# S5 rotation tables of a two-layer encoder: one outer product of two power tables in place of seven doublings

## The chip, the cores and the metric

The kernel runs on one core of one Trainium2 chip. The metric is the device time of one execution in microseconds (us). The engines are named as in the profile: PE (matrix products), DVE and POOL (elementwise work), ACT (activations and copies), SP (issues most DMAs). Each engine takes its instructions in the order in which they stand in its own queue; an instruction that waits for a semaphore holds up all that stand behind it on that engine.

## What is computed

An encoder of two layers over 800 tokens of 1024 features. Each layer mixes the tokens with three groups of heads (RG-LRU, HGRN2, S5), multiplies by w_out, and adds a squared-ReLU MLP:

```python
def linear_scan(a, b, reverse): ...            # h_t = a_t * h_{t-1} + b_t

def s5_branch(u, a_re, a_im, log_dt, b_re, b_im, c_re, c_im, d_skip, glu_w, glu_b):
    ...
    for d in range(2):
        lam = lax.complex(a_re[d], a_im[d])
        dt = jnp.exp(log_dt[d])[:, None]
        a_bar = jnp.exp(lam * dt)
        b_bar = ((a_bar - 1.0) / lam)[..., None] * lax.complex(b_re[d], b_im[d])
        bu = jnp.einsum('btgh,gph->btgp', ug, b_bar)
        h = linear_scan(jnp.broadcast_to(a_bar, bu.shape), bu, reverse=(d == 1))
        y = y + jnp.real(jnp.einsum('btgp,ghp->btgh', h, c))
    ...
# layer: x += W_out [ rms(RG-LRU) | rms(HGRN2) | rms(S5) ] * gain
#        x += relu(rms(x) W_up)^2 W_down
```

The kernel runs S5 in 100 chunks of 8 tokens. The state of each chunk is rotated by a power of a unit phasor, so that the scan over the chunks has a real decay. The powers 0 to 99 of that phasor, for 16 pairs of directions and group pairs, are the **rotation tables**.

## The kernel before

Features lie on the 128 partitions and tokens along the free dimension. The large products (`product`, L428 to L439) run as three passes of 128x128 weights over 400 tokens (L434, L435, L436), with 24 matmuls for one half of an output tile, into one of three PSUM banks (tag `mm`). Every half is evacuated by an elementwise instruction: L464 (DVE) for the products with w_in, L1123 (ACT) and L1124 (DVE) for the up products of the MLP, L1150 (DVE) for its down products. PE can't write a bank again before its evacuation has run, and with three banks it is soon that far. Weights arrive as f32 (`wr`, L446) and are split by ACT (L419) and POOL (L420, 128x1024). In the MLP, POOL also does L1129 (128x800).

`s5_setup(l)` (L706 to L874) makes the constant matrices of the S5 heads of layer l from the parameters and writes them to DRAM (TB, E, F and W). That of layer 0 is issued beside the first w_in products, between about 30 and 135 us. That of layer 1 is issued within the MLP of layer 0, after the down products of its first block (`issue_after`, L1178), and lies between about 660 and 742 us. Its parts, in order: the step's powers `PW` and the doubled powers `pw[1]`, `pw[2]` to `pw[64]` (16 columns each); the input matrices `BB`; the rotation tables; the load of the output parameters `CL` (eight DMAs, L823); `BD` and the matrices E, F and W, in which PE transposes `CL` (L836) and multiplies F (L862).

`cmul` (L725) is one complex product of elementwise instructions: four products (L726 to L729), a difference (L730) and a sum (L731). The rotation tables (L795 to L816) are made in four sets, two directions by two halves of the groups. A set has two memsets (L800, L801) for power 0, and then seven doublings: the powers n to 2n-1 are the powers 0 to n-1 times `pw[n]`, by a `cmul` on 4 x m elements (m = 1, 2, 4, 8, 16, 32, 36), 42 instructions in all. In layer 0 the last set runs on POOL and all the others run on DVE. Then two DMAs write the set (L810), and L813 to L816 make and write the scan's decay `dec`.

```python
n = 1
while n < NCH:
    m = min(n, NCH - n)
    cmul(tb[n:n+m], tb[0:m], pw[n], big, ...)   # in short
    n *= 2
```

All these tiles come from one pool, tag `t`: 11 buffers of 576 floats while the setups run. A tile that takes a buffer over waits until the last reader of its former tile is done, a DMA's landing too.

The order of the instructions on each engine is not written out by hand. A list scheduler sets it ahead of time, from the program's order with some offsets (`PR`; the setup of layer 0 has one of 400 steps) and a model of the durations. A change in the number of instructions thus moves other work in the queues, too.

Of the kernel before, what the change touches and what calls it, by code (L numbers as in the profile page):

```python
"""Two-layer bidirectional encoder trunk (RG-LRU | HGRN2 | S5 head groups, squared-ReLU MLP).

Both sequences run together with features on partitions and the 800 tokens (528 + 272, each with its 16 meta
tokens first) along the free dimension. The large products run as three float32r passes over operands split
exactly into two parts; everything else is float32. HGRN2 decays are products over dyadic intervals, so that
every factor is at most one; S5 runs in chunks of 8 tokens with a rotated real scan over the chunks.
"""
# [26 lines left out]
NCH = 100  # L34
# [9 lines left out]
# order in which the parts of a layer's mixers are issued  # L44
# [18 lines left out]
# per layer: what is moved in the issue order, pools of SBUF in their order, tiles of rs, hd, hs and ra, parts that  # L63
# take their tiles elsewhere, outputs that stay on chip, groups merged in w_out's first pass, engines
# [11 lines left out]
class Trunk:  # L76
# [14 lines left out]
    def phase(self, name, tags, tmp, bank):  # L91
        """SBUF of a phase: tag -> (floats per partition, buffers); tmp and bank: what the shared parts use."""
# [36 lines left out]
    def setup(self):  # L129
        nc = self.nc  # L130
# [15 lines left out]
        # level masks: the highest bit in which s and t differ  # L146
# [12 lines left out]
        # scores of a chunk pair, block-diagonal: the blocks beside the diagonal stay zero  # L159
# [4 lines left out]
        # what leaves the chip for a while  # L164
# [7 lines left out]
    def params(self):  # L172
        nc, ident = self.nc, self.ident
        # parameter rows of 128, transposed into columns
# [9 lines left out]
        # s5 skip gains: (g2 h) rows, (l gp) columns  # L184
        r = self.s((16, 32))
# [5 lines left out]
        # s5 step sizes over the states  # L191
# [9 lines left out]
        # lower bounds: softmax over the depth, running sum less the first  # L201
# [13 lines left out]
        # forget gate = hA*t + hB, key/2 = -hK*t + hK, with t = tanh(x/2)  # L215
# [6 lines left out]
        # rg-lru: softplus(-lambda) with log1p by its atanh series  # L222
# [23 lines left out]
    def gate_weights(self, l):  # L246
        """Block-diagonal gates: (i, d, r|i)."""
# [27 lines left out]
    def load(self):  # L275
        """The residual and the operands of the first w_in, half by half of the tokens."""
# [17 lines left out]
        for b, parts in enumerate(((0, 1, 2, 3), (4, 0, 5, 6))):  # L294
            sl = slice(b * 400, b * 400 + 400)
            # the tokens' sums of squares, from the partitions to the free dimension
# [28 lines left out]
    def final(self, m, t):  # L325
        """The last norm, feature tile by feature tile as they are done."""
# [45 lines left out]
    def split(self, k, y, gain, rs=None, n=T):  # L372
        """Operand k = y*gain (*rs) as two float32r parts that add up to it exactly."""
# [12 lines left out]
    def sumsq(self, ys, n=T):  # L386
        """The sum of squares over the partitions of all tiles, on every partition: two PSUM halves."""
# [38 lines left out]
    def product(self, w, xs, halves, evac):  # L426
        """evac(half, psum) with psum = sum over k of w[k].T @ x[k]; w: pairs of [128, 128] parts."""
# [13 lines left out]
    def fetch(self, name, l, c):  # L441
        """128 columns of a weight matrix of 1024 rows, split."""
# [8 lines left out]
    def project(self, l, cols, evacs):  # L451
        """Columns of w_in, 128 from each of cols."""
# [7 lines left out]
    def scaled(self, out):  # L460
        """Evacuation into out, times the tokens' 1/rms."""
        def ev(b, ps):
            sl = slice(b * 400, b * 400 + 400)
            self.nc.vector.tensor_tensor(out=out[:, sl], in0=ps, in1=self.r1[:, sl], op=MULT)  # L464
        return ev

    def gelu(self, x):
        """x becomes 2 gelu(x), by the tanh formula."""
# [766 lines left out]
```

## Time and profile before

| what | value |
|---|---|
| timed runs | 2216.07, 2198.86, 2207.92 us; median 2207.92 us |
| span of the profiled execution | 2201.6 us |
| PE busy | 2087.4 us, 95% of the span |
| DVE, POOL, ACT busy | 1118.9, 811.9, 753.8 us |
| PE's share of the chain that ended last | 60% |
| DVE's share of that chain | 10% |

The span of the profiled execution lies 6.3 us below the median of the timed runs, and these spread over 17 us. Times below are microseconds from the start of the profiled execution. "Pitch" means the time from the start of one instruction to that of the next on the same engine; the durations that the trace gives are longer, since neighbours overlap.

### The profile page before, as it was taken

Reading aid. Unit: us, or ns where it says so; the run is one execution under the profiler, and the core shown is the slowest. Engines: PE = TensorE matmul, PEld = TensorE weight load, DVE = VectorE, ACT = ScalarE, POOL = GpSimd, SP = SyncE. Lnnn points to the kernel's source line nnn. Section 1 sums busy time; section 2 is a strip of 40 time slices with the busy share of each in tenths; the row PEclk is TensorE's granted clock in tenths of the full one; section 3 lists DMA queues with packets and bytes.
Section 4 is the critical chain, followed back from the end, with each engine's and each line's share of the span. In section 5 each row is a group of like instructions: output and inputs, shape, how many; then the busy total and the mean of one; then the engine's idle time right before and its main releaser. Section 6 shows DMA issues by size and latency. Waiting matters only on the chain.

```text
span 2201.6 us, 34495 instructions
## 1 busy us (share of the span) xinstructions
PE 2087.4 (95%) x14082; PEld 1957.7 (89%) x14082; DVE 1118.9 (51%) x2258; ACT 753.8 (34%) x1141; POOL 811.9 (37%) x622
## 2 busy tenths in 40 slices
PE   8899899889989899999999999998998999999998
PEld 6889897677979899999998879886888999999997
DVE  6884748487657871221155855746368221112224
ACT  6233535454322232212225553436432122222222
POOL 1672112263433443333444213322434343434343
PEclk9899899899999999999999999998999999999998
DMA  5322111342211431122122113221321112122221
GB/s 182 96 81 76 38 40 56 101 129 57 68 48 58 109 119 58 58 64 61 58 95 78 57 37 97 74 59 48 113 79 58 58 58 68 59 67 65 60 67 68
DMA packets 230886, 160.74 MB, mean 73 GB/s; under 512 B 33270, under 2 KB 217784, under 8 KB 230728
## 3 DMA queue, kind: packets, MB, share of 16 engines
q1 hardware_dynamic: 229832, 156.95, 23.8%
q8 instruction: 111, 1.82, 0.4%
q10 hardware_dynamic: 896, 1.58, 0.2%
q14 instruction: 47, 0.39, 0.1%
HBM read 131.32 MB, written 27.18 MB: 72 GB/s over the span
## 4 chain that ended last, share of the span: by engine, by line
PE 60%; DVE 10%; ACT 2%; issue 1%; POOL 1%; DMA 1%; SPq 0%; DVEq 0%; POOLq 0%; ACTq 0%
PE mm L435 18%; PE mm L434 18%; PE mm L436 18%; PE hb L664 2%; PE hb L582 1%; DVE m L1163 1%; DVE h L1172 1%; PE rb L510 1%; DVE xl L379 1%; DVE m L1164 1%; DVE h L1154 1%; DVE r L1173 0%; DVE m L1124 0%; PE rb L862 0%; POOL wl L420 0%
## 5 line engine op out<-in xcount | busy, mean ns | idle before, releaser
L420 POOL TENSOR_TENSOR wl<-wr,wh 128x1024 fp32r<-128x1024 f32 (+3 forms) x214 | 479.3, 2240 | 1005.5 <-ACT wh L419 982.7
L434 PE MATMUL mm<-xh,wh 128*128 128x400 f32 (+3 forms) x2016 | 710.2, 354 | 33.1 <-DVE m L1124 11.1
L435 PE MATMUL mm<-xl,wh 128*128 128x400 f32 (+3 forms) x2016 | 713.9, 355 | 6.0 <-POOL xl L383 2.9
L436 PE MATMUL mm<-xh,wl 128*128 128x400 f32 (+3 forms) x2016 | 701.1, 349 | 0.7 <-POOL wl L420 0.5
L419 ACT ACTIVATE wh<-wr 128x1024 fp32r<-128x1024 f32 (+3 forms) x214 | 205.7, 962 | 764.9 <-PE mm L435 658.5
L434 PEld LDWEIGHTS mm<-xh,wh 128*128 128x128 f32 x2016 | 388.6, 193 | 52.7 <-DVE m L1124 14.1
L435 PEld LDWEIGHTS mm<-xl,wh 128*128 128x128 f32 x2016 | 389.1, 193 | 18.5 <-DVE xl L379 4.1
L436 PEld LDWEIGHTS mm<-xh,wl 128*128 128x128 f32 x2016 | 388.8, 193 | 8.9 <-POOL wl L420 0.9
L434 PE MATMUL mm<-u,wh 128*128 128x400 f32 (+1 forms) x1024 | 349.1, 341 | 6.2 <-DVE m L1124 6.2
L435 PE MATMUL mm<-u,wh 128*128 128x400 f32 (+1 forms) x1024 | 349.6, 341 | 0.0
L436 PE MATMUL mm<-u,wl 128*128 128x400 f32 (+1 forms) x1024 | 348.3, 340 | 0.0
L1150 DVE TENSOR_TENSOR h<-mm,h 128x400 f32<-128x400 f32 (+1 forms) x256 | 144.5, 565 | 331.2 <-PE mm L436 331.2
L1124 DVE TENSOR_TENSOR m<-m,mm 128x400 f32<-128x400 f32 (+1 forms) x128 | 71.1, 559 | 369.2 <-ACT m L1123 369.2
L434 PEld LDWEIGHTS mm<-u,wh 128*128 128x128 f32 x1024 | 193.3, 189 | 7.8 <-DVE m L1124 7.1
L435 PEld LDWEIGHTS mm<-u,wh 128*128 128x128 f32 x1024 | 193.2, 189 | 0.1
L436 PEld LDWEIGHTS mm<-u,wl 128*128 128x128 f32 x1024 | 193.1, 189 | 0.1
L1129 POOL TENSOR_TENSOR u<-m,u 128x800 fp32r<-128x800 f32 (+1 forms) x64 | 127.3, 1990 | 53.5 <-ACT u L1128 45.4
L1123 ACT ACTIVATE m<-mm 128x400 f32<-128x400 f32 (+1 forms) x128 | 62.3, 489 | 129.9 <-PE mm L436 115.8
L582 PE MATMUL hb<-hs,hs 64*64 64x64 f32 x2016 | 85.7, 236 | 8.8 <-ACT hs L615 5.6
L582 PEld LDWEIGHTS hb<-hs,hs 64*64 64x64 f32 x2016 | 72.2, 146 | 24.5 <-issue 11.4
L1128 ACT ACTIVATE u<-m 128x800 fp32r<-128x800 f32 (+1 forms) x64 | 55.1, 861 | 83.1 <-DVE m L1124 73.2
L616 DVE TENSOR_TENSOR hd<-hd,hd 128x800 f32<-128x800 f32 (+2 forms) x48 | 43.1, 902 | 13.3 <-ACT hs L614 12.8
(365 smaller groups left out, 2245.8 us busy)
## 6 DMA issues: line engine op xcount, KB each, us to landing
wr<-in_w_up_dram SPq DMA_DIRECT2D x64, 512.0 KB
wr<-in_w_down_dram SPq DMA_DIRECT2D x64, 512.0 KB
wr<-in_w_in_dram SPq DMA_DIRECT2D x46, 512.0 KB
h<-h SPq DMA_DIRECT2D x16, 400.0 KB
wr<-in_w_out_dram SPq DMA_DIRECT2D x32, 192.0 KB
TB<-t SPq DMA_DIRECT2D x24, 200.0 KB
F<-t SPq DMA_DIRECT2D x16, 256.0 KB
E<-t SPq DMA_DIRECT2D x16, 256.0 KB
```

The lines of the kernel that those rows point to most:

```text
L419: self.nc.scalar.activation(hi[:], raw, AF.Copy)
L420: self.nc.gpsimd.tensor_tensor(out=lo[:], in0=raw, in1=hi[:].bitcast(F32), op=SUB)
L434: nc.tensor.matmul(ps[:, 0:n], wh, xh[:, c0 : c0 + n], start=(k == 0), stop=False)
L435: nc.tensor.matmul(ps[:, 0:n], wh, xl[:, c0 : c0 + n], start=False, stop=False)
L436: nc.tensor.matmul(ps[:, 0:n], wl, xh[:, c0 : c0 + n], start=False, stop=(k == last))
L582: nc.tensor.matmul(ps[c % 2 * 64 : c % 2 * 64 + 64, c // 2 * 64 : c // 2 * 64 + 64], K[hr, c0 : c0 + 64], Q[hr, c0 : c0 + 64], start=True, ...
L664: mm = lambda out, w, x: nc.tensor.matmul(out, w, x, start=False, stop=False, skip_group_check=True)
L1123: nc.scalar.activation(t[:, sl], ps, AF.Relu)
L1124: nc.vector.tensor_tensor(out=t[:, sl], in0=t[:, sl], in1=ps, op=MULT)
L1128: nc.scalar.activation(u[:, 0], t[:], AF.Copy)
L1129: nc.gpsimd.tensor_tensor(out=u[:, 1], in0=t[:], in1=u[:, 0].bitcast(F32), op=SUB)
L1150: mark = nc.vector.tensor_tensor(out=t[:, sl], in0=ps, in1=t[:, sl], op=ADD)
```

## The change

In place of the doublings in each set, two tables are made once for all four sets: `P1` with the powers 0 to 7 (128x2x16x8) and `P8` with the powers 0, 8, ..., 96 (128x2x16x13). They take four memsets, four copies and five `cmul` (two for P1 with 32 and 64 elements, three for P8 with 32, 64 and 80), 30 instructions. Each set is then one `cmul` of 128 x 416 elements (4 x 13 x 8; both operands are broadcast), six instructions, of which the first 100 powers of the 104 are written to TB. The one set on POOL stays on POOL. A set now takes five buffers of tag `t` (two for the table, two for temporaries, one for `dec`) in place of four, and P1, P8 and a temporary take three more. The rest of the difference between the two files blanks comments and docstrings; lines behind L816 have numbers higher by 5.

```diff
-                tb = [self.s((128, 4, NCH)) for _ in range(2)]
-                v.memset(tb[0][:, :, 0:1], 1.0)
-                v.memset(tb[1][:, :, 0:1], 0.0)
-                big = self.s((128, 2, 256))
-                n = 1
-                while n < NCH:
-                    m = min(n, NCH - n)
-                    cmul([x[:, :, n : n + m] for x in tb], [x[:, :, 0:m] for x in tb], [x[:, ds].unsqueeze(2).to_broadcast([128, 4, m]) for x in pw[n]],
-                         [big[:, i, 0 : 4 * m].rearrange("p (a b) -> p a b", b=m) for i in range(2)], (nc.gpsimd if l == 0 and d == 1 and gq == 1 else v).tensor_tensor)
-                    n *= 2
...
+        P1, P8, tp = self.s((128, 2, 16, 8)), self.s((128, 2, 16, 13)), self.s((128, 2, 128))
+        for P, w0, w in ((P1, 1, 8), (P8, 8, 13)):
+            v.memset(P[:, 0, :, 0:1], 1.0)
+            v.memset(P[:, 1, :, 0:1], 0.0)
+            for i in range(2):
+                v.tensor_copy(P[:, i, :, 1], pw[w0][i])
+            n = 2
+            while n < w:
+                m = min(n, w - n)
+                cmul([P[:, i, :, n : n + m] for i in range(2)], [P[:, i, :, 0:m] for i in range(2)], [x.unsqueeze(2).to_broadcast([128, 16, m]) for x in pw[w0 * n]],
+                     [tp[:, i, 0 : 16 * m].rearrange("p (a b) -> p a b", b=m) for i in range(2)])
+                n *= 2
...
+                tb, tm = ([self.s((128, 4, 13, 8)) for _ in range(2)] for _ in range(2))
+                cmul([x[:] for x in tb], [P8[:, i, ds].unsqueeze(3).to_broadcast([128, 4, 13, 8]) for i in range(2)], [P1[:, i, ds].unsqueeze(2).to_broadcast([128, 4, 13, 8]) for i in range(2)],
+                     [x[:] for x in tm], (nc.gpsimd if l == 0 and d == 1 and gq == 1 else v).tensor_tensor)
```

Three places in the queues. The first is DVE in layer 0, between two evacuations (L464) of w_in's products, `mm_238` and `mm_243`; `t` are tiles of the setup. Before:

```order
L464 TENSOR_TENSOR hd_234_1155<-mm_238_1184,r1_136_454 128x400 [waits PE_49]
L726 TENSOR_TENSOR t_145_594<-t_144_591,t_138_471 128x16 [waits DVE_49]
L727 TENSOR_TENSOR t_145_594<-t_143_590,t_138_471 128x16
L729 TENSOR_TENSOR t_143_590<-t_143_590,t_138_471 128x4x4
L730 TENSOR_TENSOR t_147_644<-t_147_644,t_149_648 128x4 [waits DVE_49]
L731 TENSOR_TENSOR t_148_645<-t_148_645,t_149_648 128x4
L464 TENSOR_TENSOR hd_234_1155<-mm_243_1242,r1_136_454 128x400 [waits PE_49]
```

After the change the same two evacuations are those of `mm_245` and `mm_250`:

```order
L464 TENSOR_TENSOR hd_241_1048<-mm_245_1077,r1_136_454 128x400 [waits PE_49]
L729 TENSOR_TENSOR t_144_591<-t_144_591,t_138_471 128x16x2 [waits DVE_49]
L728 TENSOR_TENSOR t_144_591<-t_144_591,t_138_471 128x16x2 [waits DVE_49]
L729 TENSOR_TENSOR t_143_590<-t_143_590,t_138_471 128x16x4 [waits DVE_49]
L464 TENSOR_TENSOR hd_241_1048<-mm_250_1135,r1_136_454 128x400 [waits PE_49]
```

Three setup instructions stand between the two evacuations in place of five; they now belong to P1 and P8.

The second place is DVE in layer 1, around the evacuations of the first half of an up product of the MLP (`mm_1126` before, `mm_1140` after; L1124, now L1129). A wait for DMAHW is one for the landing of an earlier DMA. Before:

```order
L726 TENSOR_TENSOR t_1022_6656<-t_1021_6653,t_1007_6425 128x4 [waits DMAHW3_49]
L726 TENSOR_TENSOR t_1018_6602<-t_1017_6599,t_1009_6516 128x144 [waits DVE_49]
L727 TENSOR_TENSOR t_1018_6602<-t_1016_6598,t_1009_6516 128x144
L729 TENSOR_TENSOR t_1016_6598<-t_1016_6598,t_1009_6516 128x4x36
L727 TENSOR_TENSOR t_1022_6656<-t_1020_6652,t_1007_6425 128x4
L730 TENSOR_TENSOR t_1020_6652<-t_1020_6652,t_1022_6656 128x4 [waits DVE_49]
L731 TENSOR_TENSOR t_1017_6599<-t_1017_6599,t_1018_6602 128x4x36 [waits DVE_49]
L1124 TENSOR_TENSOR m_1125_7270<-m_1125_7270,mm_1126_7271 128x400 [waits Activation_49,Pool_49]
```

After the change, up to the evacuation of the second half:

```order
L726 TENSOR_TENSOR t_1034_6514<-t_1020_6438,t_1019_6437 128x416 [waits DMAHW2_49]
L727 TENSOR_TENSOR t_1035_6515<-t_1020_6438,t_1019_6437 128x416 [waits DVE_49]
L1129 TENSOR_TENSOR m_1139_7056<-m_1139_7056,mm_1140_7057 128x400 [waits Activation_49,Pool_49]
L728 TENSOR_TENSOR t_1033_6513<-t_1020_6438,t_1019_6437 128x416 [waits DMAHW3_49]
L729 TENSOR_TENSOR t_1032_6512<-t_1020_6438,t_1019_6437 128x416 [waits DMAHW4_49]
...
L726 TENSOR_TENSOR t_1039_6531<-t_1020_6438,t_1019_6437 128x416 [waits DVE_49]
L820 MEMSET t_1036_6524 128x4 [waits DVE_49]
L820 MEMSET t_1036_6524 128x4
L727 TENSOR_TENSOR t_1040_6532<-t_1020_6438,t_1019_6437 128x416 [waits DMAHW6_49]
L1129 TENSOR_TENSOR m_1139_7056<-m_1139_7056,mm_1141_7084 128x400 [waits Activation_49]
```

The small instructions ahead of the evacuations became few large ones; in the rows shown, four of them wait for the landings of TB writes of the sets before, in place of one.

The third place is SP in layer 0, the loads of `CL` (L823, now L828) among the TB writes of the last set, the one on POOL. Before, the eight loads end ahead of it:

```order
L823 DMA t_159_806<-in_s5_c_im_dram 128x1x64 [waits DMAHW3_49]
L823 DMA t_159_806<-in_s5_c_im_dram 128x1x64 [waits DMAHW4_49]
L446 DMA wr_343_2194<-in_w_in_dram 128x8x128 [waits DMAHW5_49,Pool_49]
L810 DMA TB0_39_157<-t_155_752 128x4x100 [waits DMAHW6_49,Pool_49]
L810 DMA TB0_39_157<-t_156_753 128x4x100 [waits DMAHW7_49,Pool_49]
```

After:

```order
L815 DMA TB0_39_157<-t_162_683 128x4x100 [waits DMAHW0_49,Pool_49]
L828 DMA t_166_699<-in_s5_c_im_dram 128x1x64 [waits DMAHW1_49]
L815 DMA TB0_39_157<-t_161_682 128x4x100 [waits DMAHW2_49,Pool_49]
L828 DMA t_166_699<-in_s5_c_re_dram 128x1x64 [waits DMAHW3_49]
L828 DMA t_166_699<-in_s5_c_re_dram 128x1x64 [waits DMAHW4_49]
L828 DMA t_166_699<-in_s5_c_im_dram 128x1x64 [waits DMAHW5_49]
L828 DMA t_166_699<-in_s5_c_im_dram 128x1x64 [waits DMAHW6_49]
L446 DMA wr_350_2087<-in_w_in_dram 128x8x128 [waits DMAHW7_49,Pool_49]
```

Five of the eight loads and the next weight load now stand behind a TB write that waits for POOL.

## Rows read from the trace of the kernel before

**Rows 1.** The page: busy times of PE; the chain that ended last.
```profile
PE 2087.4 (95%) x14082; PEld 1957.7 (89%) x14082; DVE 1118.9 (51%) x2258; ACT 753.8 (34%) x1141; POOL 811.9 (37%) x622
...
PE 60%; DVE 10%; ACT 2%; issue 1%; POOL 1%; DMA 1%; SPq 0%; DVEq 0%; POOLq 0%; ACTq 0%
```

**Rows 2.** Stretches: start:end, length, busy us (instructions) by engine, PEclk, DMA.
```profile
200.00:550.00 350.00, 318.53 (x2604) 279.10 (x2602) 226.31 (x371) 169.92 (x276) 103.86 (x138) 0.93 0.23 69
715.00:770.00 55.00, 48.76 (x258) 46.58 (x257) 49.38 (x164) 10.79 (x19) 22.75 (x17) 0.91 0.42 111
825.00:880.00 55.00, 55.00 (x304) 55.00 (x303) 9.75 (x17) 12.39 (x17) 19.98 (x9) 1.00 0.20 61
1155.00:1650.00 495.00, 473.20 (x3927) 414.32 (x3926) 295.89 (x482) 229.39 (x352) 156.14 (x157) 0.96 0.24 71
```

**Rows 3.** Waits of PE, 0 to 200 us: us in total, times, longest.
```profile
PE mm L434 <- DVE t L731: 4.4, 1, 4.4
PE rb L862 <- POOL t L730: 4.0, 4, 1.7
...
PE rb L836 <- DMA t<-in_s_c_re_dram: 2.7, 1, 2.7
```

**Rows 4.** Waits of PE, 677 to 745 us (the setup of layer 1).
```profile
PE mm L434 <- DVE m L1124: 8.7, 3, 3.7
```

**Rows 5.** Timeline of DVE in layer 0: start, length, instruction.
```profile
53.53 2.36 DVE L727 TENSOR_TENSOR t<-t,t 128x16 f32<-128x16 f32 x1
...
55.90 2.31 DVE L730 TENSOR_TENSOR t<-t,t 128x4 f32<-128x4 f32 x1
...
58.20 0.56 DVE L464 TENSOR_TENSOR hd<-mm,r 128x400 f32<-128x400 f32 x1
```

**Rows 6.** Timeline of POOL in the same place.
```profile
53.50 4.69 POOL L420 TENSOR_TENSOR wl<-wr,wh 128x1024 fp32r<-128x1024 f32 x2 [5.16 <-ACT wh L419]
```

**Rows 7.** Timeline of DVE in layer 1: two setup sets interleave.
```profile
700.43 0.42 DVE L730 TENSOR_TENSOR t<-t,t 128x256 f32<-128x256 f32 x1
700.77 0.15 DVE L726 TENSOR_TENSOR t<-t,t 128x4 f32<-128x4 f32 x1
700.84 0.15 DVE L727 TENSOR_TENSOR t<-t,t 128x4 f32<-128x4 f32 x1
...
712.48 0.30 DVE L728 TENSOR_TENSOR t<-t,t 128x144 f32<-128x144 f32 x1
712.69 0.29 DVE L726 TENSOR_TENSOR t<-t,t 128x144 f32<-128x144 f32 x1
...
713.35 0.21 DVE L728 TENSOR_TENSOR t<-t,t 128x64 f32<-128x64 f32 x1
713.49 0.21 DVE L726 TENSOR_TENSOR t<-t,t 128x64 f32<-128x64 f32 x1
...
718.69 2.44 DVE L727 TENSOR_TENSOR t<-t,t 128x144 f32<-128x144 f32 x1
```

**Rows 8.** Timeline of POOL in layer 1.
```profile
718.50 2.47 POOL L420 TENSOR_TENSOR wl<-wr,wh 128x1024 fp32r<-128x1024 f32 x1
```

**Rows 9.** Timeline of PE in layer 1: two stalls, and the matmuls behind the first.
```profile
710.33 0.70 PE L434 MATMUL mm<-xh,wh 128*128 128x400 f32 x1 [2.48 <-DVE m L1124]
...
711.49 0.54 PE L434 MATMUL mm<-xh,wh 128*128 128x400 f32 x1
711.83 0.54 PE L435 MATMUL mm<-xl,wh 128*128 128x400 f32 x1
...
722.25 0.46 PE L434 MATMUL mm<-u,wh 128*128 128x400 f32 x1 [3.71 <-DVE m L1124]
```

**Rows 10.** The chain that ended last, around 715 us: start, length, what.
```profile
714.29 2.90 DMA TB<-t
717.21 1.56 DVE t L726 x2
```

**Rows 11.** Groups of POOL by shape, 70 to 135 us: busy, mean ns.
```profile
L726 POOL TENSOR_TENSOR t<-t,t 128x144 f32<-128x144 f32 x1 | 0.4, 421 | 0.0
```

More of the change, by code (lines that the diff above doesn't have):

```diff
@@ L798, in s5_setup @@
                 ds, gs = slice(8 * d + 4 * gq, 8 * d + 4 * gq + 4), slice(4 * gq, 4 * gq + 4)
-                tb = [self.s((128, 4, NCH)) for _ in range(2)]
-                v.memset(tb[0][:, :, 0:1], 1.0)
-                v.memset(tb[1][:, :, 0:1], 0.0)
-                big = self.s((128, 2, 256))
-                n = 1
-                while n < NCH:
-                    m = min(n, NCH - n)
-                    cmul([x[:, :, n : n + m] for x in tb], [x[:, :, 0:m] for x in tb], [x[:, ds].unsqueeze(2).to_broadcast([128, 4, m]) for x in pw[n]],
-                         [big[:, i, 0 : 4 * m].rearrange("p (a b) -> p a b", b=m) for i in range(2)], (nc.gpsimd if l == 0 and d == 1 and gq == 1 else v).tensor_tensor)
-                    n *= 2
+                tb, tm = ([self.s((128, 4, 13, 8)) for _ in range(2)] for _ in range(2))
+                cmul([x[:] for x in tb], [P8[:, i, ds].unsqueeze(3).to_broadcast([128, 4, 13, 8]) for i in range(2)], [P1[:, i, ds].unsqueeze(2).to_broadcast([128, 4, 13, 8]) for i in range(2)],
+                     [x[:] for x in tm], (nc.gpsimd if l == 0 and d == 1 and gq == 1 else v).tensor_tensor)
                 for i in range(2):
-                    nc.sync.dma_start(dr["TB"][gs, :, i, d].rearrange("g p c -> p g c"), tb[i][:])
+                    nc.sync.dma_start(dr["TB"][gs, :, i, d].rearrange("g p c -> p g c"), tb[i][:].rearrange("p g a b -> p g (a b)")[:, :, 0:NCH])
                 dec = self.s((128, 4, NCH))
```

## The prediction

> **What bounds the kernel now.** I read the page first, then the waits of PE in the two setup stretches, the timelines of PE, DVE and POOL there, and last the stretches beside them. PE is busy for 2087.4 of 2201.6 us and carries 60% of the chain that ended last; DVE carries 10% of it [rows 1]. So an instruction taken off DVE is worth time only where PE waits for DVE. In most of the MLP that isn't so: from 825 to 880 us PE is busy for all 55 us, with 304 matmuls, 0.181 us apart, while DVE is busy for 9.75 us [rows 2].
>
> PE does wait in the two setups. In layer 0 there is one wait of 4.4 us for a setup instruction's queue on DVE, four of 4.0 us together for POOL before L862, and one of 2.7 us for the load of CL before L836 [rows 3]. In layer 1 there are three waits for the evacuation L1124, 8.7 us together [rows 4]: 2.48 and 3.71 us [rows 9], and so 2.5 us for the third. After a wait the matmuls start 0.34 us apart for a while [rows 9] in place of 0.181: the lower of PE's two clock levels. The stretch from 715 to 770 us shows the sum, with a mean granted clock of 0.91: 258 matmuls stand in it where a full one has 304 [rows 2], and 46 x 0.181 = 8.3 us are lost, 6.2 of them in the second and third wait and about 2 in slow matmuls.
>
> What are those evacuations late for? They stand in DVE's queue behind setup instructions. Most of these are short: two of 128x4 start 0.07 us apart. But some last over 2 us: in layer 0, L727 (128x16) takes 2.36 us from 53.53, and L730 (128x4) 2.31 us from 55.90; the evacuation comes at 58.20 [rows 5]. In the same time POOL runs two L420 from 53.50, 4.69 us together [rows 6]. In layer 1, L727 (128x144) takes 2.44 us from 718.69 [rows 7], and POOL's L420 takes 2.47 us from 718.50 [rows 8]. So a DVE instruction with two SBUF inputs that meets a weight split on POOL lasts as long as the split, whatever its own size. [...]
>
> **The change part by part.** *DVE's time.* From start to start, the trace gives 0.07 us for 128x4, 0.14 for 128x64, 0.21 for 128x144 and 0.34 for 128x256 (700.43 to 700.77) [rows 7]. Between these I estimate 0.075, 0.085, 0.10 and 0.20 for 8, 16, 32 and 128 elements. A set of doublings is then 6 x (0.07 + 0.075 + 0.085 + 0.10 + 0.14 + 0.20 + 0.21) = 5.3 us, and four are 21.1 us in layer 1 and three 15.8 us in layer 0. For 128x416 I go on along the line from 4 to 256 elements, 0.27/252 us for each: 0.34 + 160 x 0.00107 = 0.51 us. Six are 3.1 us, so four sets 12.3 us and three 9.2 us. P1 and P8 cost 12 x 0.10 + 12 x 0.14 + 6 x 0.155 = 3.8 us, and with copies and memsets about 4.2 us. DVE thus saves 21.1 - 16.5 = 4.6 us in layer 1, and 15.8 - 13.4 = 2.4 us in layer 0. If the operands broadcast along the innermost dimension cost more than this, the saving is less; no row shows it for this size, but the doublings have such operands too.
>
> *Layer 0, the evacuation.* In the order of the changed kernel, three setup instructions stand between the two L464 in place of five. Of the five, two met a split each. Two splits run back to back there, so three short instructions can meet one or both; with one, DVE is done after the first split, the second evacuation starts near 56, and the wait of 4.4 us shrinks by about 2.3. Bounds: nothing gained if both are met; 4.4 us and 2 or so of slow matmuls if none. I take -2.3.
>
> *Layer 0, POOL.* One set moves from 42 small to six large instructions on POOL. A POOL instruction of 128x144 takes 0.42 us [rows 11]; in proportion, 128x416 takes 1.2 us, and six 7.3 us, less than the small ones. The F work behind it, for which L862 waits 4.0 us [rows 3], can start earlier, so up to 4.0 us may go. Against this, five of the eight CL loads now stand on SP behind a TB write that waits for POOL's set, and L836 already waits 2.7 us for CL [rows 3]: that wait may go or may double. Bounds -6.7 and +3 us; I take -1, since POOL's set ends about when the loads went out before.
>
> *Layer 1.* The last three of the setup's evacuations matter, and DVE has only saved time by the time the third wait comes: the tables (4.2 us) are made first and the long instructions of the first sets fill the places where the cheap doublings stood. Instruction by instruction along the new order, with the prices above and the splits where POOL has them now, I get waits of 2.2, 4.2 and 0.6 us, together 7.0 in place of 8.7, or -1.7. The second wait stays because a split of 2.47 us, which ends at 720.97, falls just ahead of its evacuation [rows 8]. With the third nearly gone, part of its slow matmuls goes, -0.5. What DVE saves behind 728 us is hidden: PE there has products whose evacuations aren't late. Bounds: -8.7 - 2 = -10.7 if no wait is left, and +9 for the wait under the rivals.
>
> *The rest.* Fewer instructions move the scheduler's order in both mixing stretches: S5's first tile by some thirty matmuls earlier, late HGRN work of layer 1 by as many later. PE has 350 - 318.5 = 31.5 us idle from 200 to 550, and 495 - 473.2 = 21.8 from 1155 to 1650 [rows 2], so the order matters there, and no row says which way. I take nothing, with 10 us either way as bound, a fifth of those 53.
>
> *The sum.* -2.3 - 1 - 1.7 - 0.5 = -5.5 us: the span of 2201.6 would become 2196.1. The profiled execution lies 6.3 us below the median of 2207.9, so the time is 2202.4, say 2202.
>
> **The rivals.** *Hidden* (0.20). DVE's saving falls where no evacuation is late, and as many splits are met as before. For it: DVE is 51% busy [rows 1], and a split's price doesn't depend on the instruction's size. Against it: both bracketing evacuations in layer 0 have fewer instructions between them. Time: about 2208.
>
> *All waits go* (0.12). The 4.4 and 8.7 us and the slow matmuls behind them (2 each), and L862's 4.0: -21 us, or 2187. Against it: the splits belong to the products and still come at their pace, and DVE still has 16.5 us of setup work in layer 1.
>
> *DVE waits for its own table writes* (0.10): slower. P1 and P8 stay live and a set takes five of eleven buffers in place of four, so about one set fits at a time. Its instructions then wait, in DVE's queue, for the landings of the TB writes of the set before, and evacuations stand behind them; in layer 1 the last table instructions ahead of two evacuations wait on a DMA. Such a landing comes 2.90 us after its issue, and delays DVE once already before the change [rows 10]. If each of the five passages from set to set on DVE (three in layer 1, two in layer 0) costs 2.9 us with an evacuation behind it, and each such stall brings 2 us of slow matmuls, that is +24.5, less the 5.5: 2227. It decides from about two such passages on, 9.8 us. Against it: by the order, each of these instructions has others and an evacuation ahead of it that take longer than 2.9 us, and my replay finds the landings in time.
>
> *The mixing stretches get worse* (0.10). The late HGRN part delays the operands of w_out in layer 1, or S5's in layer 0: +10 with the -5.5, so 2212.
>
> *Durations count* (0.03). If DVE took each instruction's full length (0.15 for 128x4, 0.21 for 128x64, 0.30 for 128x144 [rows 7]) the doublings of layer 1 would cost 35 us, and the change would save about 15 us there and all waits for evacuations, 13.1 and 4 of slow matmuls: 2191. Rows 7 speak against it, with starts 0.07 apart. [...]
>
> **How the numbers follow.** My forecast, a gain of 2 to 10 us, has 0.45. The rest goes to the rivals as given. A measurement of this kernel can tell about 1%, 22 us, from no change: below 2186 is faster, above 2230 slower. The likeliest case gives 2198 to 2206 by its own terms; with the hidden one, the bad mixing and most of all waits gone, the range is 2186 to 2220. What lies under it is the rest of the good cases, about 0.10, and over it the far half of the TB waits with a bad mixing, about 0.08. Same: 0.82; faster: 0.10; slower: 0.08.
>
> **What would show it right or wrong.** In the changed profile: L726 to L731 on 128x416 about 0.51 us apart (0.55 or more refutes the size); one DVE instruction of over 2 us, not two, between the L464 near 53 and the next; PE's wait there near 2 us; three waits for the evacuation (now L1129) near 2.2, 4.2 and 0.6; no wait of DVE for TB above 1 us ahead of an evacuation; PE's idle time in the mixing stretches within 10 us of before. The prediction is wrong if DVE waits for TB writes with an evacuation behind, or if the mixing stretches move by more than the setups do.

## The result and the profile after

The changed kernel is slower: its timed runs are 2215.4 to 2239.0 us, with a median of 2234.3, against 2205.3 for the kernel before in the same comparison. The ratio is 1.0122, with an interval from 1.0077 to 1.0167. The prediction was 2202 us, with a range from 2186 to 2220, so the time lies outside the range and on the other side. The profiled execution has a span of 2213.7 us and was the fastest of its four, so its stages show 12.1 of the 29.0 us between the medians. The other three have spans of 2231.1 to 2237.3 us and a mean granted clock of PE of 0.950 to 0.953, in place of 0.962; no profile shows their stages.

The page of after, busy times and the chain that ended last, stands beside [rows 1]:

```profile
PE 2092.4 (95%) x14082; PEld 1959.6 (89%) x14082; DVE 1110.8 (50%) x2066; ACT 755.5 (34%) x1141; POOL 807.3 (36%) x586
...
PE 60%; DVE 10%; ACT 2%; issue 1%; POOL 1%; DMA 1%; DVEq 0%; SPq 0%; POOLq 0%; ACTq 0%
```

DVE has 192 instructions fewer and is busy for 8.1 us less. PE has the same number of matmuls and is busy for 5.0 us more. So the first question is in which stretch PE got slower. I cut both executions into five stages at the same places of the program: up to the last L862 of the setup of layer 0 (L867 after the change); to the first evacuation of an up product; to the first product of squares (L404) of layer 1, which contains the MLP of layer 0 and the setup of layer 1; to the first evacuation of an up product in layer 1; and the rest. The stages of after, in the columns of [rows 2]:

```profile
0.00:172.90 172.90, 153.80 (x1211) 132.51 (x1211) 132.67 (x423) 72.17 (x132) 83.11 (x83) 0.93 0.41 122
172.90:566.70 393.80, 355.93 (x2823) 316.26 (x2823) 257.06 (x409) 184.43 (x293) 115.22 (x142) 0.94 0.23 70
566.70:1165.40 598.70, 581.46 (x3168) 571.98 (x3167) 272.69 (x526) 147.89 (x207) 245.78 (x113) 0.99 0.25 74
1165.40:1653.00 487.60, 460.56 (x3797) 401.33 (x3796) 286.36 (x468) 218.16 (x337) 140.89 (x148) 0.93 0.22 67
```

The same of before, the second, third and fourth stage:

```profile
176.80:568.70 391.90, 357.81 (x2807) 317.56 (x2808) 256.79 (x408) 183.62 (x294) 114.84 (x142) 0.93 0.24 70
568.70:1171.70 603.00, 583.80 (x3172) 574.55 (x3171) 279.97 (x640) 147.73 (x207) 246.91 (x113) 0.98 0.25 74
1171.70:1640.60 468.90, 448.55 (x3795) 391.02 (x3794) 281.17 (x468) 217.28 (x337) 136.73 (x148) 0.96 0.24 69
```

| stage | before | after | difference |
|---|---|---|---|
| setup of layer 0 | 176.8 | 172.9 | -3.9 |
| mixing of layer 0 | 391.9 | 393.8 | +1.9 |
| MLP of layer 0, setup of layer 1 | 603.0 | 598.7 | -4.3 |
| mixing of layer 1 | 468.9 | 487.6 | +18.7 |
| the rest | 561.0 | 560.7 | -0.3 |
| span | 2201.6 | 2213.7 | +12.1 |

Both stages that hold the changed code got shorter, by 8.2 us together in this pair of executions (how far that goes beyond their spread is said below). The loss lies in the mixing of layer 1, 400 us behind the last changed instruction, in code that the diff doesn't touch. PE issues the same work there (3797 matmuls recorded, 3795 before) and is busy for 12.0 us longer at a granted clock of 0.93 in place of 0.96; it is idle for 27.0 us in place of 20.4. So 12.0 of the 18.7 us are slower matmuls and 6.7 are idle time.

### The profile page after: what moved, and what is told of

Read it like the earlier page. It is cut to its first block, busy times and chain, and to the rows that moved or that the text cites. A ratio compares the mean times of both kernels' runs of the same rounds, so it can differ in the third digit from the quotient of the medians.

```text
span 2213.7 us, 34278 instructions
## 1 busy us (share of the span) xinstructions
PE 2092.4 (95%) x14082; PEld 1959.6 (89%) x14082; DVE 1110.8 (50%) x2066; ACT 755.5 (34%) x1141; POOL 807.3 (36%) x586
## 4 chain that ended last, share of the span: by engine, by line
PE 60%; DVE 10%; ACT 2%; issue 1%; POOL 1%; DMA 1%; DVEq 0%; SPq 0%; POOLq 0%; ACTq 0%
PE mm L435 18%; PE mm L434 18%; PE mm L436 18%; PE hb L664 2%; DVE m L1168 1%; PE hb L582 1%; DVE h L1177 1%; PE rb L510 1%; DVE xl L379 1%; DVE m L1169 1%; DVE h L1159 1%; PE rb L948 1%; DVE r L1178 0%; DVE m L1129 0%; DVE t L730 0%
## 5 line engine op out<-in xcount | busy, mean ns | idle before, releaser
L420 POOL TENSOR_TENSOR wl<-wr,wh 128x1024 fp32r<-128x1024 f32 (+3 forms) x214 | 481.5, 2250 | 978.5 <-ACT wh L419 934.5
L434 PEld LDWEIGHTS mm<-xh,wh 128*128 128x128 f32 x2016 | 389.2, 193 | 57.7 <-DVE m L1129 14.3
L1129 DVE TENSOR_TENSOR m<-m,mm 128x400 f32<-128x400 f32 (+1 forms) x128 | 71.2, 560 | 368.6 <-ACT m L1128 368.5
L1134 POOL TENSOR_TENSOR u<-m,u 128x800 fp32r<-128x800 f32 (+1 forms) x64 | 127.2, 1988 | 52.3 <-ACT u L1133 44.4
L582 PEld LDWEIGHTS hb<-hs,hs 64*64 64x64 f32 x2016 | 73.1, 148 | 28.1 <-issue 14.0
L582 PE MATMUL hb<-hs,hs 64*64 64x64 f32 x2016 | 86.7, 238 | 11.9 <-ACT hs L615 5.6
L616 DVE TENSOR_TENSOR hd<-hd,hd 128x800 f32<-128x800 f32 (+2 forms) x48 | 46.0, 960 | 21.6 <-ACT hs L614 21.1
```

What stands on the lines that cost most here:

```text
L420: self.nc.gpsimd.tensor_tensor(out=lo[:], in0=raw, in1=hi[:].bitcast(F32), op=SUB)
L434: nc.tensor.matmul(ps[:, 0:n], wh, xh[:, c0 : c0 + n], start=(k == 0), stop=False)
L582: nc.tensor.matmul(ps[c % 2 * 64 : c % 2 * 64 + 64, c // 2 * 64 : c // 2 * 64 + 64], K[hr, c0 : c0 + 64], Q[hr, c0 : c0 + 64], start=True, ...
L616: tt(out=v(K2, 0, T + m), in0=v(K2, 0, T + m), in1=v(FP, 2 * m - 1, T - m, 0), op=MULT)
L1129: nc.vector.tensor_tensor(out=t[:, sl], in0=t[:, sl], in1=ps, op=MULT)
L1134: nc.gpsimd.tensor_tensor(out=u[:, 1], in0=t[:], in1=u[:, 0].bitcast(F32), op=SUB)
```

## Experiments

All of them ask whether the new instructions or the order of the old ones cost the time. In the texts of expectations on `evac300`, `scans_later`, `values_first` and `evac_five`, the HGRN part with a new wait is called the last one. That was misread: it is the second of the three, which is why two of these runs miss their aim (below). "Order" below is the order of the instructions in the engines' queues.

| kernel | new tables in layer | order in the mixing of layer 1 | its length, profiled | ratio to before (interval) |
|---|---|---|---|---|
| `again` | 0 and 1 | the changed one | 489.3 | 1.0110 (1.0080 to 1.0141) |
| `layer0_only` | 0 | the changed one | 500.7 | 1.0116 (1.0054 to 1.0178) |
| `layer1_only` | 1 | of before | 469.3 | 1.0000 (0.9976 to 1.0023) |
| `offset600` | 0 and 1 | of before | 472.5 | 1.0000 (0.9970 to 1.0031) |
| `offset580` | 0 and 1 | of before | 476.8 | 0.9958 (0.9937 to 0.9979) |
| `offset560` | 0 and 1 | of before | 469.1 | 0.9969 (0.9948 to 0.9990) |
| `old_offset1000` | none | a third one | 489.5 | 1.0102 (1.0069 to 1.0134) |
| `old_offset600` | none | of before | 465.0 | 1.0063 (1.0039 to 1.0086) |

**The change again, and each layer alone.** `again` is the changed kernel, unaltered. `layer1_only` puts the new tables behind `if l == 1` and the seven doublings behind `else`; `layer0_only` the other way round.

```diff
+        if l == 1:
+            P1, P8, tp = self.s((128, 2, 16, 8)), self.s((128, 2, 16, 13)), self.s((128, 2, 128))
...
+        else:
+            for d in range(2):
+                for gq in range(2):
+                    tb = [self.s((128, 4, NCH)) for _ in range(2)]
...
```

> The changed kernel once more, unaltered, for a second profile. Theory (order): in its first profile the setups gained what was forecast (the start of layer 1's mixing came 6.2 us earlier) and layer 1's mixing stretch lost 18.6 us, with PE's granted clock at 0.90 to 0.91 there; so this one is 1.010 to 1.015 of before again, and where an execution is slower than the first profile's 2213.7 us, the extra time too lies in the two mixing stretches, with less granted clock, and not in the MLP or the setups. Rival (chance): 0.997 to 1.005, the first four executions were unlucky.

> Layer 0 keeps the doublings, layer 1 gets the power tables. On all five engines the order is then that of before up to layer 1's setup, and again that of before behind it, the whole of layer 1's mixing included. Theory (order): only the setup's gain of about 2 us is left, 2203 where before has 2205, ratio 0.997 to 1.001. Rival (the new instructions cost more than they save): part of the loss stays, ratio 1.005 or more, and layer 1's setup shows it.

> Layer 0 gets the power tables, layer 1 keeps the doublings. Behind layer 1's setup the order on all five engines is that of the changed kernel. Theory (order): about 2 us slower than the changed kernel, ratio to before 1.010 to 1.016, although layer 1's setup is word for word that of before. Rival (layer 1's own new setup is at fault): ratio 0.995 to 1.001.

The change again gave 1.0110, with 489.3 us in the mixing of layer 1 and 398.7 in that of layer 0. The new tables in layer 1 alone gave 1.0000, in layer 0 alone 1.0116. The mixing of layer 1, the row of each, of `layer1_only`:

```profile
1164.70:1634.00 469.30, 450.91 (x3796) 393.59 (x3795) 281.25 (x468) 217.46 (x337) 137.60 (x148) 0.95 0.23 69
```

and of `layer0_only`, whose profiled execution was the slowest of its four:

```profile
1181.20:1681.90 500.70, 471.16 (x3796) 410.66 (x3796) 287.05 (x468) 218.58 (x338) 139.87 (x148) 0.91 0.22 65
```

So the new tables of layer 0 cost the time in the mixing of layer 1, a thousand microseconds later, and no instruction of theirs runs there. What they share with that stretch is the list scheduler: with them the order there is that of the changed kernel, without them that of before.

**The new instructions with the old order, and the old ones with another.** The offset of layer 0's setup (`su` in `PR`) moves work in the scheduler's order without an instruction added or removed. With 560, 580 or 600 in place of 400, the changed kernel gets the order of before in the mixing of layer 1. The kernel before with 1000 keeps every doubling, takes PE's order of the changed kernel in the mixing of layer 0 and a third order in that of layer 1.

```diff
-PR = [{'gh0': 1000, 'su': 400, 'hf0': -20, 'gh1': 20}, {'sf': 400, 'rc2': -400, 'hi0': -60, 'hc2': 150}]
+PR = [{'gh0': 1000, 'su': 580, 'hf0': -20, 'gh1': 20}, {'sf': 400, 'rc2': -400, 'hi0': -60, 'hc2': 150}]
```

> The changed kernel with the priority offset of layer 0's setup at 600 in place of 400; every instruction of both setups is the changed kernel's. Layer 0 gets an order of its own; behind layer 1's setup the order on all five engines is that of before. Theory (order): layer 1's mixing takes what it took before, and the kernel is 2 to 8 us faster than before, ratio 0.996 to 1.000, unless layer 0's new order costs something. Rival (the new instructions, not the order): 1.010 to 1.015 like the changed kernel.

> The changed kernel with the priority offset of layer 0's setup at 580 in place of 400. All instructions are the changed kernel's, but on PE the order of both mixing stretches is that of before. Theory (order): both setups keep their gain, layer 0's mixing takes about 391 us as with the doublings and layer 1's, from the first statistics product to the first up evacuation, 469 to 473 as before and not 488; ratio to before 0.994 to 0.999. Rival (the tables themselves cost what is lost, or layer 0's gain was spent in its own order): ratio 1.000 to 1.012.

> The kernel before, doublings in both layers, with that offset at 1000. On PE, layer 0's mixing stretch then has the order that the changed kernel has; layer 1's has a third order, in which, as in the changed kernel, the four scans of an S5 group stand on DVE ahead of the evacuation that the transposes of the last HGRN part wait for. Theory (order): with no new instruction at all the kernel gets slower than before: layer 0's mixing 394 to 401 us in place of 391, a wait of 3 to 4 us at those transposes with slow matmuls behind it, ratio 1.003 to 1.015. Rival (the new instructions): ratio 0.998 to 1.002.

`offset600` measured 1.0000, `offset580` 0.9958 and `old_offset1000` 1.0102. Three stages missed what was expected. In `offset580` the mixing of layer 1 took 476.8 us (expected 469 to 473) and that of layer 0 398.3 (about 391); in `old_offset1000` that of layer 0 took 380.3 (394 to 401). The setup stage ahead of it ended at 163.7 us in the one and at 190.5 in the other. The mixing of layer 1 of `offset580`:

```profile
1161.20:1638.00 476.80, 457.69 (x3797) 398.32 (x3796) 281.17 (x468) 217.15 (x338) 137.63 (x148) 0.94 0.23 68
```

and of `old_offset1000`:

```profile
1173.50:1663.00 489.50, 465.75 (x3795) 407.46 (x3794) 285.95 (x468) 218.66 (x337) 136.52 (x148) 0.91 0.22 66
```

This separates the two. The old instructions in a different order lose 1.0%, about as much as the change does. The new instructions in the order of before lose nothing, and with 580 they gain 0.4%, 9 us. The stage shows it in all profiles: the seven kernels with the order of before take 465.0 to 476.8 us in the mixing of layer 1, and the six with the changed order or one close to it 486.3 to 500.7.

**Is the offset alone the gain?** It could be that 560 to 600 is simply a better place for the setup. So the kernel before ran with 600, and the changed one with a third value, 560 (the edits are again the number in `PR`).

> The control for the offset: the kernel before, doublings in both layers, with the offset of layer 0's setup at 600. Both mixing stretches and all behind them keep the order of before on all engines; only the setup of layer 0 lies otherwise beside the first products. Theory (with the order held, the tables are worth 4 to 10 us, and the offset by itself little): ratio 0.998 to 1.002. Rival (the offset alone made the kernel with 580 faster): ratio 0.994 to 0.997.

> The changed kernel with that offset at 560: both mixing stretches in the order of before on PE, and layer 0's setup placed a little otherwise than with 580. Theory (order held, tables worth 4 to 10 us): ratio 0.994 to 0.999, as with 580. Rival (580 was a lucky placing of layer 0's setup): 1.000 or more.

The offset with the old tables costs 0.6%, which I hadn't expected, and its profiled execution, the fastest of its twelve, doesn't show it: a span of 2200.3 us against 2201.6. Why the other runs are slower stays open; the order of both mixing stretches is that of before, so that order isn't all that sets the time. At 560 the new tables give 0.9969. So at 600 the offset alone is no gain: the kernel is 0.6% slower there with the old tables than with the new ones. With the new ones 560 and 580 agree on a gain. The old tables at 560 and 580 weren't tried, so how much of this gain is the tables' and how much the place of layer 0's setup isn't shown. Of the 14 us by which the profiled execution of `offset560` (2187.5) is shorter than that of before, 11.4 lie in the setup and the mixing of layer 0 (557.3 in place of 568.7) and 3.7 in the stage with the setup of layer 1 (599.3). The kernels with 560 and 580 are faster than both that this case began with, by 0.3 to 0.4% than the one before.

**What in the changed order costs?** The waits of PE in the mixing of layer 1 give a first candidate. Of after (us in total, times, longest):

```profile
PE hb L565 <- DVE hs L464: 6.3, 2, 3.9
PE rb L404 <- POOL rs L394: 4.5, 2, 2.4
PE rb L510 <- DVE rs L501: 3.5, 1, 3.5
...
PE hb L644 <- ACT hs L570: 2.0, 1, 2.0
PE rb L948 <- POOL rs L940: 1.8, 1, 1.8
```

The same of before:

```profile
PE rb L510 <- DVE rs L501: 3.1, 1, 3.1
...
PE hb L565 <- DVE hs L464: 2.5, 1, 2.5
PE rb L404 <- POOL rs L394: 2.1, 1, 2.1
```

One wait of 3.9 us is new: HGRN's transposes (L565) of the second part wait for an evacuation (L464). It is in all kernels with the changed order or the third one (3.7 to 3.9 us) and in none with the order of before. The timeline of DVE in after shows what it is late for (start, length, instruction):

```profile
1385.15 1.82 DVE L609 TENSOR_TENSOR hd<-hd,hs 128x1600 f32<-128x1600 f32 x1
1387.47 3.70 DVE L930 TENSOR_TENSOR_SCAN rs<-rs,rs 128x100 f32<-128x100 f32 x4 [0.51 <-POOL rs L923]
1391.10 0.54 DVE L464 TENSOR_TENSOR hs<-mm,r 128x400 f32<-128x400 f32 x1
```

and POOL beside it:

```profile
1388.10 2.34 POOL L420 TENSOR_TENSOR wl<-wr,wh 128x1024 fp32r<-128x1024 f32 x1
```

In the changed order, S5's four scans stand ahead of that evacuation, and a weight split falls on them, so that they take 3.70 us. In before they run behind the evacuation and take 1.53:

```profile
1371.31 0.57 DVE L464 TENSOR_TENSOR hs<-mm,r 128x400 f32<-128x400 f32 x1 [1.35 <-PE mm L436]
...
1375.69 1.53 DVE L925 TENSOR_TENSOR_SCAN rs<-rs,rs 128x100 f32<-128x100 f32 x4 [0.74 <-POOL rs L918]
```

This is the price that the prediction gave a DVE instruction that meets a split [rows 5 to 8], met by a scan. To test what the wait is worth, four kernels try to move something at it: `scans_later` holds back the scans of that S5 group by two POOL instructions that multiply by 1.0, `evac300` ranks the evacuations of layer 1's projections higher by an offset of 300 (`pe`), `values_first` projects the values of the last HGRN part ahead of its queries, and `evac_five` repeats an evacuation of the last part in the kernel before.

```diff
+                for _ in range(2 if l == 1 and gp == 3 else 0):
+                    nc.gpsimd.tensor_scalar(out=v(AB, 100), in0=v(AB, 100), scalar1=1.0, scalar2=None, op0=MULT)
```

```diff
-PR = [{'gh0': 1000, 'su': 400, 'hf0': -20, 'gh1': 20}, {'sf': 400, 'rc2': -400, 'hi0': -60, 'hc2': 150}]
+PR = [{'gh0': 1000, 'su': 400, 'hf0': -20, 'gh1': 20}, {'sf': 400, 'rc2': -400, 'hi0': -60, 'hc2': 150, 'pe': 300}]
```

```diff
+        if l == 1 and i == 2:
+            self.project(l, (XI + 128 * i, XQ + 128 * i), (self.scaled(V), self.scaled(Q)))
```

```diff
+            for _ in range(4+1 if late and b == 1 else 1):
```

> The changed kernel with two extra POOL products by 1.0 (128x200, about 0.3 us each) behind the POOL sums of one S5 group in layer 1. On PE the order stays the changed kernel's but for a few rows; on DVE two of that group's four scans now stand behind the evacuation for which the transposes of the last HGRN part wait. Theory (that wait costs itself and slow matmuls behind it): the wait falls from 3.8 us to 2 or less, layer 1's mixing takes 480 to 486 us in place of 488 to 490, ratio 1.005 to 1.010. Rival (the wait is only a mark of the order, the loss is spread over many places): 1.010 to 1.013 as the changed kernel.

> The changed kernel with the evacuations of layer 1's w_in products moved up by 300 priority steps. Layer 0's mixing is that of the changed kernel; layer 1's order lies about half way between that of before and that of the changed kernel, and the scans still stand ahead of the last HGRN evacuation. Theory (order): that wait stays, 3 to 4 us, others go; layer 1's mixing takes 475 to 490 us, ratio 1.002 to 1.012. If it takes 469 or less, the wait at the transposes isn't what costs.

> The changed kernel, where the last HGRN part of layer 1 projects its values ahead of its queries. The transposes of the values then needn't wait for the last evacuation; the rest of layer 1's order stays within 1.4 matmuls of the changed kernel's on average. Theory (that wait): it goes, and layer 1's mixing takes 475 to 484 us, ratio 1.002 to 1.009, unless the scores wait for the queries instead. Rival (spread): 1.010 to 1.013.

> The kernel before, with the same evacuation (last HGRN part of layer 1, second half of the values) done five times over; nothing else moves on any engine. It makes the transposes wait for about 4 x 0.49 = 2.0 us where they now wait for less than 0.3. Theory: layer 1's mixing takes the 2 us and 1 to 5 us of slow matmuls more than before, 472 to 476 us, ratio 1.001 to 1.003. Rival (PE has slack there): ratio 0.999 to 1.001 and 469 us.

`scans_later` did what it was built for: the wait fell to 1.6 us, in the waits of PE of that kernel:

```profile
PE hb L565 <- DVE hs L464: 4.1, 2, 2.5
```

The 2.5 is the other wait, which before has too. But the mixing of layer 1 took 486.3 us, against 487.6 and 489.3 in the two executions of the changed kernel, and the ratio is 1.0092 (1.0064 to 1.0121). That ratio lies in the range of the theory (1.005 to 1.010), and the stage just above its range (480 to 486). Still, with the wait 2.3 us shorter, 17.4 of the 18.7 us are left, so the wait isn't what makes most of the loss. What it is worth by itself isn't settled: one order differs by more than 3 us from execution to execution, and 1.6 us of the wait are still there. The 0.3 us that were expected for each of the two POOL products are an estimate, and no row here shows them; L924, on POOL and of 128x200 too, takes 0.61 us in after. A loss spread over many places of the new order is the rival that is left, argued and not tested. `evac300` (1.0099, 1.0067 to 1.0131) kept the changed order's wait of 3.7 us and took 492.7 us, a little above what was expected. `values_first` (1.0095, 1.0064 to 1.0127) and `evac_five` (1.0011, 0.9989 to 1.0034) act on the third part, where no such wait is: the wait stayed at 3.7 us in the one, and in the other none arose at PE. They say nothing on it.

**Where the loss is spread.** It lies mainly between the last gate product and the last score product of that stage. Before:

```profile
1316.50:1524.00 207.50, 201.58 (x1999) 179.51 (x2000) 132.10 (x240) 85.32 (x162) 57.87 (x94) 0.98 0.24 71
```

After:

```profile
1312.20:1540.10 227.90, 214.25 (x2025) 189.61 (x2026) 138.48 (x237) 90.66 (x167) 65.82 (x96) 0.92 0.22 67
```

Of the 20.4 us there, 12.7 are PE's busy time, at a clock of 0.92 in place of 0.98, and 7.7 idle time. A small part is work that changed places: 26 more matmuls are recorded between these two points than before. Waits and slow clock go together in parts of it, but not in all (last section): behind the wait of 3.9 us the granted clock is 0.50 from 1392 to 1396 us.

## Why the prediction was wrong, step by step

**The size of the new instructions** was right. In layer 1 the 128x416 instructions start 0.50 us apart (predicted 0.51). Two take longer: one of 2.32 us beside POOL's L1134 (128x800, 2.09 us from 713.72), and one of 2.70 beside a split (L420, 2.69 us from 715.76):

```profile
707.35 0.58 DVE L726 TENSOR_TENSOR t<-t,t 128x416 f32<-128x416 f32 x1
707.86 0.58 DVE L727 TENSOR_TENSOR t<-t,t 128x416 f32<-128x416 f32 x1
...
713.93 2.32 DVE L730 TENSOR_TENSOR t<-t,t 128x416 f32<-128x416 f32 x1
716.20 2.70 DVE L726 TENSOR_TENSOR t<-t,t 128x416 f32<-128x416 f32 x1
...
719.33 0.56 DVE L1129 TENSOR_TENSOR m<-m,mm 128x400 f32<-128x400 f32 x1
```

On POOL the six take 7.0 us together, predicted 7.3.

**Layer 1** was right in its mechanism and its waits. The waits of PE from 677 to 760 us, in place of [rows 4]:

```profile
PE mm L434 <- DVE m L1129: 6.6, 3, 4.1
```

Singly they are 2.13, 4.11 and 0.37 us; I had 2.2, 4.2 and 0.6. The second comes from the two long rows above, behind which L1129 stands at 719.33. The stage gained 4.3 us in place of 2.2, since PE's busy time fell by 2.3, and not by the 0.5 that I gave the slow matmuls. This term is the same in every kernel with new tables in layer 1: the stage takes 598.6 to 599.4 us there, and 602.7 to 603.4 without them.

**Layer 0, the evacuation and POOL.** I had -2.3 and -1, and the stage gained 3.9 in this execution, but by other pieces. Both splits fell behind the evacuation, as my better bound had it, though by 0.18 us only:

```profile
51.53 0.57 DVE L464 TENSOR_TENSOR hd<-mm,r 128x400 f32<-128x400 f32 x1
52.02 2.15 DVE L726 TENSOR_TENSOR t<-t,t 128x64 f32<-128x64 f32 x1
54.09 2.45 DVE L727 TENSOR_TENSOR t<-t,t 128x64 f32<-128x64 f32 x1
```

and POOL's two splits beside them:

```profile
51.71 4.74 POOL L420 TENSOR_TENSOR wl<-wr,wh 128x1024 fp32r<-128x1024 f32 x2 [5.16 <-ACT wh L419]
```

So the wait of 4.4 us in [rows 3] went, and the four of L862 went too. What became late in their place stands in the waits of PE from 0 to 200 us:

```profile
PE hb L582 <- DVE hn L595: 4.5, 1, 4.5
...
PE rb L841 <- DMA t<-in_s_c_re_dram: 2.4, 1, 2.4
```

HGRN's scores (L582) wait 4.5 us, until 115.65, for an evacuation of scores on DVE (L595). Ahead of it in DVE's queue stand an HGRN product (L616) that meets a split on POOL (2.36 us from 105.61) and takes 2.60 us, where it takes 0.97 at 115.77 with nothing on POOL, and setup instructions of 128x256 that start about 0.82 us apart, beside setup work of 128x288 on POOL (0.85 us each at 110.70 and at 111.52):

```profile
106.21 2.60 DVE L616 TENSOR_TENSOR hd<-hd,hd 128x800 f32<-128x800 f32 x1
...
110.95 0.90 DVE L727 TENSOR_TENSOR t<-t,t 128x256 f32<-128x256 f32 x1
111.76 0.89 DVE L728 TENSOR_TENSOR t<-t,t 128x256 f32<-128x256 f32 x1
...
115.34 0.17 DVE L595 COPY_PREDICATED hn<-mk,hb 16x32 f32<-16x32 int32 x1
```

In [rows 7] such an instruction of 128x256 takes 0.34 us to the next one. But before the change some of them met the same work on POOL (0.97 us at 111.08, 0.85 at 112.02) and took as long:

```profile
111.43 0.90 DVE L726 TENSOR_TENSOR t<-t,t 128x256 f32<-128x256 f32 x1
112.26 0.90 DVE L727 TENSOR_TENSOR t<-t,t 128x256 f32<-128x256 f32 x1
```

So the meeting isn't new; new is that these scores stand behind it in the queue, another price of the order. This is read from the rows and wasn't tested. The load of `CL` is late by 2.4 us where it was 2.7.

The 3.9 us of the stage are 2.3 of PE's idle time and 1.6 of its busy time, with 12 matmuls fewer recorded in it, so they aren't simply the waits that went less the one that came. Nor are they clear of the spread. With the doublings and the order of before in layer 0, this stage takes 176.8 us in before, 174.5 in `layer1_only` and 172.9 in `evac_five`:

```profile
0.00:172.90 172.90, 152.55 (x1223) 133.02 (x1223) 138.41 (x502) 72.32 (x132) 93.01 (x119) 0.95 0.41 122
```

With the new tables at an offset of 400 it takes 171.4 to 176.6 us in six kernels. Setup and mixing of layer 0 together take 563.9 to 568.7 us in the first three and 566.7 to 578.1 in these six. So no gain of the setup of layer 0 is shown there, and the changed order of that layer's mixing probably costs some us as well.

**DVE waits for its own table writes** was rightly held unlikely. From 660 to 745 us DVE has one group of waits, and it is for PE:

```profile
DVE h L1155 <- PE mm L436: 18.0, 11, 1.8
```

The wait for such a landing is on POOL in layer 0, 10.8 us ahead of its set, and no evacuation stands behind it there.

**The rest** is the step that failed: "Fewer instructions move the scheduler's order in both mixing stretches [...] I take nothing, with 10 us either way as bound, a fifth of those 53." The order did move, and it cost 20.6 us in this execution (18.7 + 1.9) and 27.2 in that of `again` (20.4 + 6.8). Two things were wrong with the bound. It was made from PE's idle time alone, and that grew by 6.7 + 3.8 = 10.5 us, about as far as the bound went. The other half, 12.0 - 1.9 = 10.1 us, is busy time: the same matmuls at a lower clock (0.93 in place of 0.96 in layer 1). I had read in the setups that slow matmuls come behind a wait (0.34 us apart in place of 0.181 [rows 9]), and had priced them there, and left them out here. And the middle of a bound was taken as the forecast, though the bound was wider than all the other terms of the sum together. The rival on the mixing stretches, 2212 us at a chance of 0.10, had the right place of the loss by stage and half its size. Of the places it named within, w_out's operands in layer 1 aren't where the loss is: behind the last score product that stage takes 112.9 us, and 116.6 before. No row was read for S5's tile of layer 0.

**From the profile to the time.** The sum's last step was mis-sized too: I put the median 6.3 us above the profiled span, as before, and it lies 20.6 above that of after (2234.3 and 2213.7). So of the 32 us between forecast and median, about 20.6 are the mixing stretches and 14.3 this step, less 2.7 by which the setups gained more than I had. The other timed runs have no profile. The one of `again` is 7.3 us longer than that of after, and 6.6 of them lie in the two mixing stretches; that fits the lower clock of those runs, but doesn't show where their time went.

Shown by the runs: the setup of layer 1 gains about 4 us; the order of the mixing of layer 1 is what costs most, some 20 us; with the order of before there the change costs nothing, and the kernel gains 0.3 to 0.4% at two offsets. Not shown: a gain of the setup of layer 0 at the offset of 400; which of the many shifts in the new order make up the loss (one wait was shortened, and most of the loss stayed); why the tables of layer 0 change the scheduler's order in layer 1 while those of layer 1 don't; and why `old_offset600` is slower than its order says.

## What to carry to other kernels

Where a scheduler sets the order, a change has two prices, that of its instructions and that of the order that it happens to bring; the second was over twice the first in the two profiles here, and lay 400 us behind the last changed line. Forecast it from a bound that counts slow matmuls beside waits, and where that bound is wider than the rest of the sum, put the chances by it. In measuring, hold the order (another offset, one part of the change alone) before judging the instructions, and profile an order more than once: one order took 487.6 to 500.7 us for one stage in three of them. The same tables are 1.2% slower or 0.4% faster than before, by one number in a table of offsets.

## What the runs showed of the chip

**A busy PE at half its clock.** Of the 4403 stretches of 0.5 us in the profile of before, 4062 have a granted clock of 1.00 and 291 one of 0.50; each of the other 50 lies between one of 1.00 and one of 0.50. In after they are 4067, 309 and 51 of 4427. So these two levels are all that the two traces show. From 711 to 713 us in before, where the matmuls behind the first wait start 0.34 us apart [rows 9], the clock is 0.50. In `again` PE shows no idle time from 1460 to 1480 us, and yet its granted clock falls from 1.00 to 0.50 (stretches of 4 us, in the columns of [rows 2]):

```profile
1460.00:1464.00 4.00, 4.00 (x52) 3.55 (x50) 2.42 (x7) 0.00 (x0) 1.59 (x6) 1.00 0.42 104
1464.00:1468.00 4.00, 4.00 (x35) 3.02 (x33) 0.00 (x0) 0.60 (x1) 0.00 (x0) 0.83 0.24 75
1468.00:1472.00 4.00, 4.00 (x25) 3.73 (x26) 0.00 (x0) 1.01 (x3) 0.00 (x0) 0.50 0.00 0
1472.00:1476.00 4.00, 4.00 (x20) 3.33 (x19) 0.00 (x0) 0.67 (x3) 0.00 (x0) 0.50 0.02 4
```

What PE did before is a run of small state products (L664), without a large product from 1458.32 to 1470.85. Two of its rows, ahead of the fall and behind it, 14 matmuls of one form each time:

```profile
1464.96 1.02 PE L664 MATMUL hb<-hd,hd 64*64 64x64 f32 x14
...
1467.88 1.75 PE L664 MATMUL hb<-hd,hd 64*64 64x64 f32 x14
```

In the profile of after, the same order at the same place loses the clock later and for a shorter time:

```profile
1468.00:1472.00 4.00, 4.00 (x43) 3.48 (x42) 0.00 (x0) 0.39 (x2) 0.00 (x0) 1.00 0.01 4
1472.00:1476.00 4.00, 4.00 (x22) 3.39 (x20) 0.00 (x0) 1.30 (x4) 0.00 (x0) 0.57 0.02 4
```

The kernel before has a run of small products too, from 1449.07 to 1462.78, and keeps a clock of 1.00 through it and behind it. So which runs cost the clock isn't settled by these rows. They show a fall without any idle time of PE in the profile (in which the ends of matmuls are modelled), and that the place of the fall can differ by some microseconds between executions of one order.

**A scan beside a split took longer, too.** Four scans of 128x100 took 1.53 us with no split beside them and 3.70 beside a split of 2.34: 2.2 us longer, about the length of the split.
